# An RMSNorm input laid out twice: a second copy of x with channels on partitions replaces the transposes of three of four token blocks

## The chip, the cores and the metric

One core of a Trainium2 chip. The metric is device time in microseconds of one execution of the kernel; the time of the kernel before is the median of 3 runs.

## The reference

One layer of a streaming-encoder trunk on x of 2048 tokens by 1024 channels, in float32:

```
xn = rmsnorm(x, norm1_g)                  # x * rsqrt(mean(x*x) + 1e-6) * g, per token
z  = xn @ w_in                            # 4608 columns: pool, HGRN2 q / f / i / o, two branch gates
ya = pool_mixer(u) @ w_pa ;  yb = hgrn2(q, f, i, o) @ w_pb
x  = x + (gates_a * ya + gates_b * yb) @ w_o
x  = x + conv_glu_ffn(rmsnorm(x, norm2_g), w_up, conv_w, conv_b, w_down)
return rmsnorm(x, final_g)
```

What matters here is the first line: each token is scaled by its own factor (rstd), each channel by its gain, and the product is needed with channels on partitions, since the projection sums over channels.

## The kernel before, in words

**Blocks.** The tokens are cut into four blocks of 512 (0 to 3), and two blocks make a super-block of 1024 that goes through the mixer and then the FFN (loop at the end of `tile_trunk`, `b` = 0 and 2). The large products over a super-block are done with seven half-size products instead of eight (P1 to P7). Their operands are sums and differences of quarters of the input: B11 and B21 are the first block's channels 0 to 511 and 512 to 1023; T1 to T4 and B22 are formed from both blocks. `forms_a_task` makes B11 and B21 of the even block, `forms_b_task` makes T1 to T4 and B22 of the odd one.

**Precision.** Every operand is split in a high and a low half in fp32r (`split`, L587: high half by ACT L597 or POOL L595, low half by DVE L598), and three matmuls of 128x512 stand for one product. Weights are converted the same way by `stream` (ACT L205, DVE L206), from eight raw buffers that SP loads.

**The input operands.** `load_rows` loads a block as four row tiles of 128 tokens, each in two halves of 512 channels (8 DMAs of 256 KB on SP). `norm_rows` takes a row tile's squares and their sums on ACT (`row_rstd`, L626), the factor rstd on POOL (L627, L619, L620), and multiplies both halves by it on DVE into x_xs (L640). Then 128x128 transposes on PE (L646) bring x_xs into PSUM, 32 for a block. In the even block ACT copies each 128x512 result times the gain into x_b (L654); in the odd block ACT makes -B22 (L714) and DVE the differences t1, t2 and t3 straight from PSUM (`minus`, L703), four each. In block 0 (`early`) the transposes follow row tile by row tile; all others come as the operands are due.

**What sets the order.** The forms are tasks that are stepped once in six matmuls, and the framework's scheduler then fixes one static order for each engine when the kernel is built. An engine carries out its queue in that order: an instruction that waits holds up all behind it. The names: io_X, io_Y, io_Z and io_V are PSUM results of the first part of the input projection (the products with B11, B21, T2 and so on; x_f0 to x_f7 are the split B11 and B21 of the even block); dn_P is the FFN's last product, whose operands dn_P_0h to dn_P_10h and their low halves are cast by ACT (L597) and DVE from tiles g_P. The last product of a super-block (P3, operands 0 to 10) is the work beside which the rows of the next two blocks are loaded and normalised (`X_AT`, `X_AT2` in `ffn`). Tiles come from one pool of 77 slots of 128x528, so a tile's DMA waits until its slot is free.

Of the kernel before, what the change touches and what calls it, by code (L numbers as in the profile page):

```python
# [29 lines left out]
TB = 512  # L30
NT = TB // P
# [26 lines left out]
M_ORDER = (0, 4, 1, 5, 2, 6, 3, 7)  # L58
# [20 lines left out]
def tile_trunk(  # L79
# [10 lines left out]
    w_dn: bass.AP,  # L90
    params: bass.AP,
    final_g: bass.AP,
    out: bass.AP,
):
    nc = tc.nc
    pe, act, dve, pool, sp = nc.tensor, nc.scalar, nc.vector, nc.gpsimd, nc.sync

    const = ctx.enter_context(tc.tile_pool(name="const", bufs=1))
# [395 lines left out]
    xt = {}  # L494
    ready = set()

    def load_x_tile(b, j):
        for c in range(2):
            t = slot(f"x{b}_{j}_{c}")
            r = b * TB + j * P  # L500
            sp.dma_start(t, x[r : r + P, 512 * c : 512 * c + 512])
            xt[("x", b), j, c] = t
        ready.add((("x", b), j))

    def load_rows(b):
        for j in range(NT):
            load_x_tile(b, j)


    load_x_tile(0, 0)  # L510

    ident = const.tile([P, P], F32, tag="ident", name="ident")
# [18 lines left out]
    def col(o):  # L531
        return cols[:, o : o + 1]

    negs = const.tile([P, 16], F32, tag="negs", name="negs")
    pool.tensor_scalar(negs, cols[:, :16], -1.0, None, ALU.mult)

    neghalf = const.tile([P, 4], F32, tag="neghalf", name="neghalf")
    pool.memset(neghalf, -0.5)
# [78 lines left out]
    def rstd_of(ssq, n, scale, name):  # L617
        r = small.tile([P, 4], F32, tag="rstd", name=name)
        pool.tensor_scalar(r[:, :n], ssq, scale, EPS, ALU.mult, ALU.add)  # L619
        pool.tensor_tensor(r[:, :n], r[:, :n], neghalf[:, :n], ALU.pow)  # L620
        return r

    def row_rstd(halves, junk, name):
        ss = small.tile([P, 4], F32, tag="ssq", name=name + "ss")
        for hf in range(2):
            act.activation(junk[hf], halves[hf], AF.Square, accum_out=ss[:, hf : hf + 1])  # L626
        pool.tensor_tensor(ss[:, 2:3], ss[:, 0:1], ss[:, 1:2], ALU.add)  # L627
        return rstd_of(ss[:, 2:3], 1, 1.0 / D, name + "r")

    def norm_rows(src, name, xs, after, lag=1):  # L630
        for j in range(NT):
            while (src, j) not in ready:
                yield 1
            halves = [xt[src, j, c] for c in range(2)]
            t = [slot(f"{name}xs{j}_{hf}") for hf in range(2)]
            r = row_rstd(halves, t, f"{name}{j}")
            if lag:
                yield lag
            for hf in range(2):
                dve.tensor_scalar(t[hf], halves[hf], r[:, 0:1], None, ALU.mult)  # L640
                xs[j, hf] = t[hf]
            after(j)
# [5 lines left out]
    def transposed(xs, k, name, gain, ps=None):  # L648
        if ps is None:
            ps = bank(f"{name}t{k}")  # L650
            for j in range(NT):
                transpose(ps, xs, j, k)
        t = slot(f"{name}b{k}")
        act.activation(t, ps, AF.Copy, scale=col(gain + k))  # L654
        return t
# [10 lines left out]
    def forms_a_task(src, gain, forms, full, after=lambda j: None, early=False):  # L666
        name = f"{src[0]}{src[1]}_"
        xs = {}
        pts = [bank(f"{name}t{k}") for k in range(KD)] if early else [None] * KD

        def rows(j):
            after(j)
            if early:
                for k in range(KD):
                    transpose(pts[k], xs, j, k)

        yield from norm_rows(src, name, xs, rows)
        yield 6
        for k in range(KD):
            t = transposed(xs, k, name, gain, pts[k])  # L680
            yield 1
            key = "B11" if k < 4 else "B21"
            full[key].append(t)
            forms[key].append(split(t, f"{name}f{k}", True))

    def forms_b_task(src, gain, forms, full, after, go):
        name = f"{src[0]}{src[1]}_"
        xs = {}
        yield from norm_rows(src, name, xs, after, 0)
        while not go():  # L690
            yield 2
        t1, b12, b22 = [], [], []

        def turned(k):
            ps = bank(f"{name}t{k}")
            for j in range(NT):
                transpose(ps, xs, j, k)
            return ps

        def minus(key, k, ps, x1, c=None, op=ALU.subtract):  # L700
            t = slot(f"{name}{key}{k}")
            c = gain + (k if c is None else c)
            dve.scalar_tensor_tensor(t, ps, col(c), x1, ALU.mult, op)  # L703
            return t


        t3 = []
        for k in range(4):
            while len(full["B11"]) <= k:
                yield 4  # L710
            p12 = turned(k)
            p22 = turned(k + 4)
            t = slot(f"{name}b{k}")
            act.activation(t, p22, AF.Copy, scale=negs[:, gain + k + 4 : gain + k + 5])  # L714
            b22.append(t)
            t1.append(minus("t1", k, p12, full["B11"][k]))
            t2 = minus("t2", k, p22, t1[k], k + 4)
# [797 lines left out]
    for _ in range(5):  # L1515
        nxt[1].step()
    load_rows(1)
    join(nxt[1])
    Task(setup_task())
# [63 lines left out]
```

## Time and profile before

| | us |
|---|---|
| median of 3 runs | 2624.07 |
| lowest, highest | 2617.74, 2628.94 |
| the profiled execution | 2626.91 |
| its span | 2625.2 |

The span runs from the first to the last instruction; 1.7 us of the profiled execution lie around it. In that execution the granted TensorE clock was 0.987 in the mean. PE was busy for 2537.5 us (97%) of the span, DVE for 1977.9 (75%), ACT for 1170.8 (45%), POOL for 913.0 (35%). Of DMA, 496.90 MB were moved, 189 GB/s in the mean.

How to read the rows in the next sections. A row of a timeline has the start in microseconds from the span's start, the time until its group ended, the engine, the line, the operation, its output and inputs with their shapes, and xN for N such instructions in a row; in brackets stands how long the engine was idle ahead of it and what it waited for. A row of waits has engine, tile and line that waited, the releaser, the total in us, the number of waits and the longest. A row of one line's instructions has the least, median and greatest duration in ns. SPq is SP's queue of DMA issues; its rows give the time of issuing, not of landing.

### The profile page before, as it was taken

What the parts mean: (1) busy time and instruction counts of PE and PEld (TensorE: products, weight loads), DVE (VectorE), ACT (ScalarE), POOL (GpSimd) and SP (SyncE); (2) the same over time, 40 slices, a digit from 0 to 9 for tenths busy, and PEclk for the clock granted to TensorE, in tenths of its full rate; (3) what the DMA queues carried; (4) which work ended last, traced back from release to release, by engine and by line L of the source; (5) the groups of instructions that cost most, each with busy time, mean ns of one, the idle gap of its engine ahead of it and who ended that gap; (6) DMA issues with size and microseconds to landing.
All of it is one profiled execution on the core that took longest, in us unless ns stands there. A gap on an engine that the chain in (4) does not pass through costs nothing. (4 is left out here: it accounts for less than half of the span.)

```text
span 2625.2 us, 35598 instructions
## 1 busy us (share of the span) xinstructions
PE 2537.5 (97%) x11464; PEld 2065.1 (79%) x11464; DVE 1977.9 (75%) x3390; ACT 1170.8 (45%) x2204; POOL 913.0 (35%) x1253
## 2 busy tenths in 40 slices
PE   7899999998999999999999999999999999999998
PEld 6688877777778888878878788888787888887887
DVE  7888779458789877877376787775778887777845
ACT  5334334313655454455364344443345454444633
POOL 6544344042444433353141111210623433335402
PEclk8999999999999999999999999999999999999999
DMA  6787759988768897488364344346452444445942
GB/s 213 271 223 205 204 181 245 267 263 209 217 184 244 239 235 211 148 299 282 98 206 159 97 125 133 109 153 213 149 166 88 151 151 148 141 140 182 378 142 105
DMA packets 254059, 496.90 MB, mean 189 GB/s; under 512 B 26736, under 2 KB 43248, under 8 KB 253552
## 3 DMA queue, kind: packets, MB, share of 16 engines
q1 hardware_dynamic: 187968, 319.89, 38.3%
q0 software_dynamic: 41504, 110.64, 16.5%
q10 hardware_dynamic: 24400, 64.08, 7.0%
q8 instruction: 91, 1.49, 0.2%
q14 instruction: 96, 0.79, 0.1%
HBM read 384.94 MB, written 187.17 MB: 218 GB/s over the span
## 5 line engine op out<-in xcount | busy, mean ns | idle before, releaser
L205 ACT CAST ops<-raw 128x512 fp32r<-128x512 f32 x732 | 451.5, 620 | 819.7 <-PE dn_P L145 140.0
L206 DVE TENSOR_TENSOR ops<-raw,ops 128x512 fp32r<-128x512 f32 x732 | 565.2, 776 | 205.3 <-ACT ops L205 194.3
L1375 DVE SCALAR_TENSOR_TENSOR e<-h,cols,e 128x512 f32<-128x512 f32 x176 | 142.6, 813 | 30.2 <-ACT e L1373 26.1
L1373 ACT ACTIVATE e<-h,cols 128x512 f32<-128x512 f32 x176 | 142.5, 814 | 24.2 <-DVE h L978 16.9
L1378 DVE SCALAR_TENSOR_TENSOR e<-h,cols,e 128x512 f32<-128x512 f32 x176 | 133.9, 769 | 3.0
L796 POOL DMA_DIRECT2D g_P<-dg_P x154 | 83.7, 545 | 107.6 <-PE dn_P L145 69.4
L1084 POOL TENSOR_TENSOR gf_P<-e,e 128x512 f32<-128x512 f32 x44 | 67.9, 1545 | 152.9 <-DVE e L1384 97.5
L1295 POOL TENSOR_TENSOR ya<-ya,gl 128x512 f32<-128x512 f32 x32 | 46.8, 1490 | 107.7 <-DVE gl L1287 107.7
L1084 POOL TENSOR_TENSOR gf_P<-gf_P,e 128x512 f32<-128x512 f32 x44 | 60.2, 1368 | 68.0 <-DVE e L1384 67.5
L1368 POOL COPY h<-h 128x2 f32<-128x2 f32 x88 | 40.7, 481 | 114.3 <-DVE h L976 112.3
L1370 POOL COPY hist<-h 128x2 f32<-128x2 f32 x88 | 35.3, 401 | 125.9 <-DVE h L978 124.2
L1382 ACT ACTIVATE e<-e 128x512 f32<-128x512 f32 x88 | 55.6, 631 | 38.8 <-DVE e L1378 38.4
L1191 POOL TENSOR_TENSOR q<-q,qs 128x512 f32<-128x512 f32 x16 | 21.9, 1366 | 141.6 <-ACT qs L1190 72.9
L978 DVE TENSOR_TENSOR h<-up_u,up_V 128x512 f32<-128x512 f32 x88 | 60.1, 684 | 13.6 <-PE up_V L145 13.1
L1228 ACT ACTIVATE gt<-gt,cols 128x512 f32<-128x512 f32 x48 | 34.8, 725 | 77.4 <-DVE gt L978 63.5
L845 POOL COPY qm<-q 128x64 f32<-128x64 f32 x64 | 24.9, 410 | 117.3 <-DVE q L910 31.2
L1060 DVE TENSOR_TENSOR x<-x,wo_P 128x512 f32<-128x512 f32 x88 | 56.6, 689 | 8.2 <-PE wo_P L145 8.2
L1060 DVE TENSOR_TENSOR ac<-ac,dn_P 128x512 f32<-128x512 f32 x72 | 46.6, 684 | 13.4 <-PE dn_P L145 13.3
L1398 POOL DMA_DIRECT2D dg_P<-gf_P x88 | 52.5, 596 | 10.8 <-POOL gf_P L1084 6.5
L853 PE MATMUL pl<-qm,k 128*128 128x192 f32 x256 | 48.2, 331 | 6.1 <-DVE qm L849 3.8
L1444 POOL TENSOR_TENSOR fss<-fss 128x1 f32<-128x1 f32 x16 | 4.6, 288 | 142.0 <-ACT fj L1433 142.0
L853 PEld LDWEIGHTS pl<-qm,k 128*128 128x128 f32 x256 | 43.3, 191 | 10.4 <-ACT qm L844 3.4
(1265 smaller groups left out, 8283.6 us busy)
## 6 DMA issues: line engine op xcount, KB each, us to landing
g_P<-dg_P POOLq DMA_DIRECT2D x154, 256.0 KB, 6.4
raw<-in_w_up_t SPq DMA_DIRECT2D x132, 256.0 KB, 3.2
raw<-in_w_in_t SPq DMA_DIRECT2D x98, 256.0 KB, 3.2
dg_P<-gf_P POOLq DMA_DIRECT2D x88, 256.0 KB, 3.9
raw<-in_w_io SPq DMA_DIRECT2D x68, 256.0 KB, 5.1
dg_P<-e SPq DMA_DIRECT2D x66, 256.0 KB, 3.3
raw<-in_w_dn SPq DMA_DIRECT2D x66, 256.0 KB, 3.0
x<-in_x SPq DMA_DIRECT2D x64, 256.0 KB, 5.3
```

The costliest lines, as they stand in the source:

```text
L205: self.mark = act.copy(hi, v)
L206: dve.tensor_tensor(lo, v, f32(hi), ALU.subtract)
L796: eng.dma_start(t, d)
L853: pe.matmul(pa_[:, c * 192 : c * 192 + 192], ks[:, (i + c) * P : (i + c + 1) * P], mv[:, c].rearrange("p s x -> p (s x)"), start=True, sto ...
L978: dve.tensor_tensor(dst, t, ps, ALU.add if how == "add" else ALU.subtract)
L1060: dve.tensor_tensor(t, t, ps[j], ALU.add if sg > 0 else ALU.subtract)
L1084: pin(pool.tensor_tensor(t, x0, x1, op))
L1373: in_turn(act.activation(t, h[:, 2:], AF.Identity, bias=col(o_cb + mt), scale=col(o_cw + 4 * MF + mt)))
L1375: in_turn(second(dve.scalar_tensor_tensor(t, h[:, 1 : 1 + TB], col(o_cw + 2 * MF + mt), t, ALU.mult, ALU.add)))
L1378: dve.scalar_tensor_tensor(t, h[:, 0:TB], col(o_cw + mt), t, ALU.mult, ALU.add)
L1382: in_turn(act.activation(g, g, AF.Silu))
L1398: pool.dma_start(d, t)
```

## The change

A second copy of x, transposed on the host ahead of the launch, comes in as the input xc (1024 channels by 2048 tokens). For blocks 1, 2 and 3 `load_rows` also loads the block's eight tiles of 128 channels by 512 tokens (256 KB each), behind the rows. The rows are still loaded, but only for the squares, which now overwrite them. `norm_cols` takes the place of `norm_rows`: from each row tile's rstd, DVE makes a diagonal 128x128 tile (x_di = identity times rstd), PE multiplies a matrix of ones by it (x_rb, fp32), so that each partition holds the 128 factors of the tokens, and when all four are there ACT copies x_rb (128x512) to SBUF as x_rbs. DVE then scales each xc tile in place by the channel's gain and x_rbs. In the even block 2 that is the operand itself; in the odd blocks t1, t2 and t3 are formed from scaled tiles in SBUF, t3 in place, by DVE. Gone for these blocks are x_xs, the transposes (32 a block), ACT's x_b, and the reads of PSUM. Block 0 and the FFN's own norm (m) are unchanged.

```diff
+    ones = const.tile([P, P], F32, tag="ones", name="ones")
+    pool.memset(ones, 1.0)
...
     def load_rows(b):
         for j in range(NT):
             load_x_tile(b, j)
+        if b:
+            for k in M_ORDER if b % 2 else range(KD):
+                t = slot(f"xc{b}_{k}")
+                sp.dma_start(t, xc[k * P : (k + 1) * P, b * TB : (b + 1) * TB])
+                xct[b, k] = t
...
+    def norm_cols(src, name, lag=1):
+
+        ps = bank(f"{name}rb")
+        for j in range(NT):
+            while (src, j) not in ready:
+                yield 1
+            halves = [xt.pop((src, j, c)) for c in range(2)]
+            r = row_rstd(halves, halves, f"{name}{j}")
+            if lag:
+                yield lag
+            t = slot(f"{name}di{j}")[:, :P]
+            dve.tensor_scalar(t, ident, r[:, 0:1], None, ALU.mult)
+            pe.matmul(ps[:, j * P : (j + 1) * P], ones, t, start=True, stop=True)
+        rb = slot(f"{name}rbs")
+        act.copy(rb, ps)
+        return rb
...
     def forms_a_task(src, gain, forms, full, after=lambda j: None, early=False):
...
-        yield from norm_rows(src, name, xs, rows)
-        yield 6
+        rb = None
+        if src[0] == "x" and not early:
+            rb = yield from norm_cols(src, name)
+        else:
+            yield from norm_rows(src, name, xs, rows)
+            yield 6
         for k in range(KD):
-            t = transposed(xs, k, name, gain, pts[k])
+            if rb is None:
+                t = transposed(xs, k, name, gain, pts[k])
+            else:
+                t = xct.pop((src[1], k))
+                dve.scalar_tensor_tensor(t, t, col(gain + k), rb, ALU.mult, ALU.mult)
...
     def forms_b_task(src, gain, forms, full, after, go):
...
-        yield from norm_rows(src, name, xs, after, 0)
+        if src[0] == "x":
+            rb = yield from norm_cols(src, name, 0)
+        else:
+            yield from norm_rows(src, name, xs, after, 0)
...
             else:
-                t3.append(minus("t3", k, p12, b22[k], op=ALU.add))
+                x12, t = (xct.pop((src[1], k + c)) for c in (0, 4))
+                dve.scalar_tensor_tensor(x12, x12, col(gain + k), rb, ALU.mult, ALU.mult)
+                dve.scalar_tensor_tensor(t, t, negs[:, gain + k + 4 : gain + k + 5], rb,
+                                         ALU.mult, ALU.mult)
+                b22.append(t)
+                t1.append(slot(f"{name}t1{k}"))
+                dve.tensor_tensor(t1[k], x12, full["B11"][k], ALU.subtract)
+                t2 = slot(f"{name}t2{k}")
+                dve.scalar_tensor_tensor(t2, t, -1.0, t1[k], ALU.mult, ALU.subtract)
+                dve.tensor_tensor(x12, x12, t, ALU.add)
+                t3.append(x12)
...
+        "xc": a["x"][0].T,
```

The static orders differ from those of before only near the start and near the boundary between the two super-blocks. Three places follow. Line numbers of the changed kernel are 1 to about 50 higher (L206 is L205 of before, L608 is L597, L637 is L626, L682 is L654).

ACT at the start, before, from its fifth cast of weights on (ops<-raw is a weight's high half, x_b an operand of block 0, x_0_0 to x_3_1 in the squares are the row tiles and halves of block 1):

```order
L205 CAST ops_392<-raw_106 128x512
L654 ACTIVATE x_b_230<-x_t_130,cols 128x512
L205 CAST ops_409<-raw_108 128x512
L654 ACTIVATE x_b_236<-x_t_131,cols 128x512
L654 ACTIVATE x_b_242<-x_t_132,cols 128x512
L654 ACTIVATE x_b_248<-x_t_133,cols 128x512
L654 ACTIVATE x_b_254<-x_t_134,cols 128x512
L654 ACTIVATE x_b_260<-x_t_135,cols 128x512
L205 CAST ops_420<-raw_110 128x512
L654 ACTIVATE x_b_266<-x_t_136,cols 128x512
L205 CAST ops_439<-raw_112 128x512
L654 ACTIVATE x_b_272<-x_t_137,cols 128x512
```

The same place after the change, from the sixth cast on:

```order
L206 CAST ops_426<-raw_108 128x512
L637 ACTIVATE x_0_0_216,x_0ss<-x_0_0_216 128x512
L637 ACTIVATE x_0_1_218,x_0ss<-x_0_1_218 128x512
L682 ACTIVATE x_b_248<-x_t_132,cols 128x512
L637 ACTIVATE x_1_0_220,x_1ss<-x_1_0_220 128x512
L637 ACTIVATE x_1_1_222,x_1ss<-x_1_1_222 128x512
L637 ACTIVATE x_2_0_224,x_2ss<-x_2_0_224 128x512
L682 ACTIVATE x_b_254<-x_t_133,cols 128x512
L637 ACTIVATE x_2_1_226,x_2ss<-x_2_1_226 128x512
L637 ACTIVATE x_3_0_228,x_3ss<-x_3_0_228 128x512
L637 ACTIVATE x_3_1_230,x_3ss<-x_3_1_230 128x512
L682 ACTIVATE x_b_260<-x_t_134,cols 128x512
```

The squares of block 1, which stood behind all eight x_b of block 0, now stand ahead of the first and between the next ones; on POOL the statistics of block 1 likewise moved between the splits x_f0h, x_f1h and x_f2h.

ACT at the boundary, before (dn_P_6h and dn_P_7h are operands of the last FFN product of the first super-block; the squares are those of block 2):

```order
L205 CAST ops_12496<-raw_12179 128x512
L597 CAST dn_P_6h<-g_P_6_12164 128x512
L626 ACTIVATE x_xs_0_12378,x_0ss<-x_0_0_12347 128x512
L626 ACTIVATE x_xs_1_12379,x_0ss<-x_0_1_12349 128x512
L626 ACTIVATE x_xs_0_12395,x_1ss<-x_1_0_12351 128x512
L205 CAST ops_12561<-raw_12208 128x512
L626 ACTIVATE x_xs_1_12396,x_1ss<-x_1_1_12353 128x512
L597 CAST dn_P_7h<-g_P_7_12187 128x512
```

And after, from the third row tile of block 2 to that of block 3's end:

```order
L637 ACTIVATE x_2_1_12330,x_2ss<-x_2_1_12330 128x512
L608 CAST dn_P_6h<-g_P_6_12137 128x512
L637 ACTIVATE x_3_0_12332,x_3ss<-x_3_0_12332 128x512
L637 ACTIVATE x_3_1_12334,x_3ss<-x_3_1_12334 128x512
L608 CAST dn_P_7h<-g_P_7_12160 128x512
L608 CAST dn_P_8h<-g_P_8_12166 128x512
```

dn_P_6h stood ahead of all squares of block 2 and now stands behind the sixth of the eight, with dn_P_7h and dn_P_8h behind the last.

ACT a little later, after the change (x_rbs is of block 2, the squares are of block 3):

```order
L655 COPY x_rbs<-x_rb 128x512
L206 CAST ops_12707<-raw_12365 128x512
L637 ACTIVATE x_0_0_12465,x_0ss<-x_0_0_12465 128x512
L637 ACTIVATE x_0_1_12467,x_0ss<-x_0_1_12467 128x512
L637 ACTIVATE x_1_0_12469,x_1ss<-x_1_0_12469 128x512
L637 ACTIVATE x_1_1_12471,x_1ss<-x_1_1_12471 128x512
L637 ACTIVATE x_2_0_12473,x_2ss<-x_2_0_12473 128x512
L637 ACTIVATE x_2_1_12475,x_2ss<-x_2_1_12475 128x512
L637 ACTIVATE x_3_0_12477,x_3ss<-x_3_0_12477 128x512
L608 CAST dn_P_9h<-g_P_9_12243 128x512
L637 ACTIVATE x_3_1_12479,x_3ss<-x_3_1_12479 128x512
```

Before, dn_P_9h stood ahead of block 3's squares and dn_P_10h behind the eighth; now dn_P_9h is behind the seventh, and dn_P_10h follows the copy x_rbs of block 3. On PE dn_P_10's matmuls moved behind the first matmuls of io_X, and x_rb's four stand between dn_P_6 and dn_P_8 for block 2 and from dn_P_9 on for block 3. On SP, block 2's eight xc loads stand between the rows of block 2 and five raw weights, and block 3's rows and xc tiles stand behind three more raw weights (kw0ioP to kw2ioP); before, block 3's rows stood behind one.

More of the change, by code (lines that the diff above doesn't have):

```diff
@@ L92, in tile_trunk @@
     final_g: bass.AP,
+    xc: bass.AP,
     out: bass.AP,
@@ L503, in load_x_tile @@
         ready.add((("x", b), j))
+    xct = {}
     def load_rows(b):
@@ L710, in forms_b_task @@
                 yield 4
[L711 to L717, printed above, removed]
-            if src[0] == "m":
+            if src[0] == "m":
+                p12 = turned(k)
+                p22 = turned(k + 4)
+                t = slot(f"{name}b{k}")
+                act.activation(t, p22, AF.Copy, scale=negs[:, gain + k + 4 : gain + k + 5])
+                b22.append(t)
+                t1.append(minus("t1", k, p12, full["B11"][k]))
+                t2 = minus("t2", k, p22, t1[k], k + 4)
                 t = slot(f"{name}t3{k}")
@@ L722, in forms_b_task @@
             else:
-                t3.append(minus("t3", k, p12, b22[k], op=ALU.add))
+                x12, t = (xct.pop((src[1], k + c)) for c in (0, 4))
+                dve.scalar_tensor_tensor(x12, x12, col(gain + k), rb, ALU.mult, ALU.mult)
+                dve.scalar_tensor_tensor(t, t, negs[:, gain + k + 4 : gain + k + 5], rb,
+                                         ALU.mult, ALU.mult)
+                b22.append(t)
+                t1.append(slot(f"{name}t1{k}"))
[4 more added lines that the diff above has]
+                t3.append(x12)
             forms["T2"].append(split(t2, f"{name}T2{k}"))
```

## The prediction

> **What bounds the kernel now.** I read the page first, then busy time by stretch, PE's waits in two of the stretches, then those places instruction by instruction.
>
> ```profile
> span 2625.2 us, 35598 instructions
> PE 2537.5 (97%) x11464; PEld 2065.1 (79%) x11464; DVE 1977.9 (75%) x3390; ACT 1170.8 (45%) x2204; POOL 913.0 (35%) x1253
> PE   7899999998999999999999999999999999999998
> PEclk8999999999999999999999999999999999999999
> ```
> ```profile
> 7.60:130.00 122.40, 106.32 (x443) 84.64 (x444) 105.20 (x138) 55.75 (x108) 73.89 (x90) 0.93 0.71 243
> 1320.00:1390.00 70.00, 64.70 (x299) 52.45 (x298) 56.30 (x90) 44.16 (x99) 28.79 (x48) 0.95 0.58 195
> ```
>
> PE is busy for 97% of the span, so what counts is PE's queue and its few waits. In the second fence the columns are length, then PE, PEld, DVE, ACT and POOL busy, granted clock, DMA share and GB/s. Those two stretches (the start, and the boundary between the super-blocks) lose 16.1 and 5.3 us of PE time and have the low clocks. All transposes of x lie in them, so the change is priced there. PE's waits in the first, then in the second:
>
> ```profile
> PE x_t L646 <- DVE x_xs L640: 8.7, 3, 7.6
> PE io_Z L145 <- DVE io_u L1129: 3.8, 1, 3.8
> PE x_t L646 <- DVE x_t L703: 3.6, 2, 2.1
> PE io_X L145 <- POOL x_f0h L595: 2.4, 1, 2.4
> PE io_Z L145 <- DVE x_t L703: 1.5, 1, 1.5
> ```
> ```profile
> PE dn_P L145 <- ACT dn_P_10h L597: 3.6, 1, 3.6
> PE dn_P L145 <- ACT dn_P_7h L597: 1.0, 1, 1.0
> ```
>
> 7.6 of the 8.7 us is the wait before PE's first instruction. The transposes of block 1 then cost waits of 1.1 + 3.6 + 1.5 = 6.2 us. The wait for io_u comes later in the start, and is a wait for DVE whatever PE did before.
>
> **What the change takes off PE.** 96 transposes of the 128 of x (block 0 keeps 32).
>
> ```profile
> 1361.66 1.04 PE L646 MATMUL x_t<-ident,x_xs 128*128 128x128 f32 x8
> 1362.45 0.71 PE L145 MATMUL io_Y<-ops,x_f5h 128*128 128x512 f32 x2
> L892 PE MATMUL pl<-q,k x256: 270/275/461, 147.1 to 1725.5; 128*128 128x128 f32 x128
> ```
>
> Eight take (1362.45 - 1361.66) = 0.79 us of queue, 0.1 each, so 96 are 9.5 us. Twelve matmuls x_rb come in. The nearest row is the fp32 128x128 matmul pl (median 275 ns, neighbours overlapping): between 0.1 and 0.27 each, 1.2 to 3.3 us; I take 0.12, the transpose's end, since a lone transpose has the same duration (0.27 us). So PE has 8 us less to do. That is a gain only where PE gets its operands sooner.
>
> **The start.**
>
> ```profile
> 13.97 0.68 ACT L654 ACTIVATE x_b<-x_t,cols 128x512 f32<-128x512 f32 x1
> 15.06 3.00 ACT L654 ACTIVATE x_b<-x_t,cols 128x512 f32<-128x512 f32 x5
> 10.73 5.06 SPq L501 DMA_DIRECT2D x<-in_x  x8
> x<-in_x SPq DMA_DIRECT2D x64, 256.0 KB, 5.3
> 17.17 1.04 POOL L595 TENSOR_SCALAR x_f2h<-x_b 128x512 fp32r<-128x512 f32 x1
> 16.67 2.07 PE L145 MATMUL io_X<-ops,x_f0h 128*128 128x512 f32 x4 [2.41 <-POOL x_f0h L595]
> 29.43 0.62 PE L145 MATMUL io_Y<-ops,x_f4h 128*128 128x512 f32 x2
> 40.56 1.47 PE L646 MATMUL x_t<-ident,x_xs 128*128 128x128 f32 x12
> 52.22 1.22 PE L145 MATMUL io_Z<-ops,x_T20h 128*128 128x512 f32 x2 [1.53 <-DVE x_t L703]
> ```
>
> In the new order two squares of block 1 stand on ACT ahead of block 0's first x_b, and six more among the next ones. They wait for DMAs: the second load is issued at about 10.7 + 0.65 and lands 5.3 later, at 16.7. With its square (0.6) x_b starts at 17.4 instead of 13.97, and x_f0h, 1.04 on POOL, ends at about 19.2: the first matmul of io_X comes at 19.2 for 16.67, **2.5 us later**. Then PE has half of io_X (24 matmuls) and stands before x_rb, whose x_di is on DVE behind x_f7l. POOL makes the eight splits of 1.04 and, between them, three more rows' statistics (about 1 us each): 18.1 + 11.3 = 29.5, and x_f7l 0.7 more: 30.2. PE waits about 3 us there. A matmul takes (40.56 - 29.43)/48 = 0.232 at full clock; after a wait the first four took 2.07, 0.52 each, so the clock is halved and some 1.7 us more go. The rest of io_X (5.6 + 1.7 + 0.7 for x_rb and the step in) ends at 38.2, io_Y 11.1 later at 49.4, for 40.56. From here the gain: the stretch from 40.56 to 52.22, 11.7 us of transposes and their waits, is gone, and io_Z starts at about 49.4 rather than 52.22.
>
> The Trainium skill (TensorE: Matmul & The Clock Gate, Part 1) has the clock fall only after an idle window of about 3.4 us. By that my 3 us wait costs no half clock, and the sum would be 1.7 us less; the row after a 2.41 us wait (0.52 each) speaks against it.
>
> PE's lead of 3 us is not kept, for DVE sets the end of this stretch.
>
> ```profile
> L703 DVE SCALAR_TENSOR_TENSOR x_t<-x_t,cols,x_b x8: 736/742/746, 43.4 to 55.5; 128x512 f32<-128x512 f32 x8
> L640 DVE TENSOR_SCALAR x_xs<-x,x_0r x4: 480/484/487, 7.1 to 37.7; 128x512 f32<-128x512 f32 x4
> L206 DVE TENSOR_TENSOR ops<-raw,ops x16: 678/680/1764, 11.7 to 127.7; 128x512 fp32r<-128x512 f32 x16
> 92.09 1.19 PE L145 MATMUL io_Z<-ops,x_T40h 128*128 128x512 f32 x2 [3.79 <-DVE io_u L1129]
> ```
>
> Off DVE go 8 x_xs (0.48) and 12 L703 (0.74): 12.7 us. On it come 4 x_di (not in the trace; between 0.1 and 0.48 as they have a quarter of x_xs's columns; 0.2 taken), 12 scalar_tensor_tensors at 0.74 and 8 tensor_tensors at 0.68: 15.1. So DVE has 2.4 us more, of which the 0.08 that starts overlap take some 1. Its place for the eight scalings is after x_rbs (ACT's copy, about 36.7), and it idles from 31 to there, as it idled about as long at 22 to 31 before. Contention adds some more (rival 2). So io_u, and PE at 92.09, come 1.5 us later; PE's wait of 3.8 grows by its lead. Bounds: -3 if the scalings fit into DVE's idle time, +5 if a third of the 20 operations take the 1.76 us that the L206 row has as its maximum. **Start: +1.5 us.**
>
> ```profile
> 16.17 3.58 SPq L182 DMA_DIRECT2D raw<-in_w_io  x6
> 31.09 1.29 POOL L338 TENSOR_TENSOR w8s<-raw,raw 128x512 f32<-128x512 f32 x1
> ```
>
> On SP's queue the eight loads of xc stand ahead of these six raw weights, which land 5.4 us later: the first at 16.2 + 5.3 + 5.4 = 26.9, the last at 30.5. Their first reader, w8s, ran at 31.09, so this is hidden by less than a microsecond; w8s itself moves behind the later x_f7h in any case.
>
> **The boundary.**
>
> ```profile
> 1318.58 0.62 ACT L597 CAST dn_P_6h<-g_P 128x512 fp32r<-128x512 f32 x1
> 1322.51 0.63 ACT L626 ACTIVATE x_xs<-x 128x512 f32<-128x512 f32 x1 [3.32 <-DMA x<-in_x]
> 1341.18 0.60 ACT L597 CAST dn_P_10h<-g_P 128x512 fp32r<-128x512 f32 x1
> 1320.67 3.55 SPq L501 DMA_DIRECT2D x<-in_x  x5
> 1323.33 2.03 PE L145 MATMUL dn_P<-ops,dn_P_6h 128*128 128x512 f32 x8
> 1341.84 3.78 PE L145 MATMUL dn_P<-ops,dn_P_10h 128*128 128x512 f32 x8 [3.60 <-ACT dn_P_10h L597]
> 1375.36 0.71 PE L145 MATMUL io_Z<-ops,x_T20h 128*128 128x512 f32 x2 [0.30 <-DVE x_t L703]
> ```
>
> Before, the cast dn_P_6h stood ahead of block 2's squares and was done at 1319.2; dn_P_10h stood behind all squares of block 3, and PE waited 3.60 us for it. Now dn_P_6h stands behind the sixth square of block 2, dn_P_9h behind the copy x_rbs and seven squares of block 3.
> - dn_P_6h: the sixth load is the third of the five from 1320.67 on, issued at about 1322.1 and landed 5.3 later, 1327.4 to 1327.7. Square and cast: PE starts dn_P_6 at 1328.9 for 1323.33. That is 5.6 us of waiting, and half clock behind it (8 in 3.78 against 8 in 2.03): 1.7.
> - dn_P_6 to 8 are 36 matmuls, 8.4, with the 1.7 and four x_rb: PE is through at about 1339.6.
> - dn_P_9h: x3's rows are loaded behind the eight new loads of xc (256 KB, 3.55/5 = 0.7 each): 5.4 us later. Block 3's squares ended at 1341.18, so the eighth would end at 1346.6, the seventh at 1346, and PE starts dn_P_9 at about 1346.5: 6.9 us of waiting, 1.7 of half clock. Its low half stands on DVE behind the eight scalings of block 2, which x_rbs releases at about 1337: done by 1343, so ACT is the later one. The raw weights of the next projection, also 5.4 us later, are first used behind io_X's start and stay hidden.
> - dn_P_9 and dn_P_10, io_X, io_Y: 24 + 96 matmuls, 27.9; with 1.7 and 0.5 for x_rb, io_Z starts at 1376.6.
> Before, 1375.36: **boundary +1.2 us**. Bounds: -9 if the squares never hold the casts (5.6 + 6.9 + 2 x 1.7 gone, and DVE's eight scalings, 5.3, late instead); +6 if x3's loads also wait for raw buffers that PE frees late, or the half clock lasts twice as long.
>
> Elsewhere ACT loses 16 x_b and POOL nothing; ACT is 45% busy and hides that. The 6 MB more of DMA lie in these two places.
>
> **Sum.** +1.5 + 1.2 = +2.7 on the profiled execution: 2625.2 + 2.7, and the 1.7 us that lay around the span, make 2629.6. That execution was 2.8 above the median of 2624.07, so on the median's scale it is 2626.8; I give 2628, between.
>
> **Rivals.**
> 1. *The squares hold up nothing* (the loads land sooner, or casts find operands ready). For it: ACT is idle 55% of the time. Against: ACT waited 3.32 us for the very load of x. Then the boundary is -9 and the start -3: 2612 to 2615. Chance 0.10 for over 0.5% faster (13 us, about what a measurement tells from no change).
> 2. *DVE and POOL collide*, the slower side. Before, L703 read one operand from PSUM; all 20 new operations of a b-block read two from SBUF. L206, which does so too, takes 0.68, but 1.76 at most. POOL makes its sums of weights in just that stretch of the start. If each of block 1's 20 pays 1.08, PE at 92.09 is 21 us later: 2648. It decides from 10 of the 20 on (+11 beside the 2.7). Chance 0.12.
> 3. *Boundary at its upper bound*, +6: 2634. Chance 0.10; it lies within 0.5%.
>
> The Trainium skill (SBUF — State Buffer, Who interferes with whom) has a Vector instruction with two SBUF inputs and a GpSimd instruction that reads SBUF exclude each other for a whole instruction. By that rule each of the 20 that meets a POOL sum pays, as rival 2 has it; the median of 0.68 says that most do not meet one.
>
> The forecast itself has 0.68. Faster 0.10, the same 0.78, slower 0.12. The range reaches from rival 1's upper edge to most of rival 2's: 2613 to 2644.
>
> **What would show it.** Right: 5 to 6 us of PE waiting for dn_P_6h and 6 to 7 for dn_P_9h, with ACT waiting for x's DMA ahead of both; no wait of 3.6 for dn_P_10h; io_X starting 2.5 us later and io_Z about 3 earlier in the start; PE's wait for io_u above 3.8. Wrong: x_b at 14 as before, or xc's scalings well over 0.74 each, or a gain over 5 us, which would mean that the orders on ACT cost nothing.

## The result, and the profile after

The changed kernel takes 2648.28 us (median of 6 runs) where the kernel before takes 2627.42 (median of 6): the ratio is 1.0083, with a 95% interval from 1.0069 to 1.0097. Forecast were 2628 us and no change that can be measured; the time lies 4 us above the top of the range. The profiled execution took 2647.6 us, and its span is 20.7 us longer than that of before.

The page of the changed kernel, the span, the busy times and the rows of PE and its clock:

```profile
span 2645.9 us, 35450 instructions
PE 2537.2 (96%) x11392; PEld 2061.2 (78%) x11392; DVE 1979.4 (75%) x3402; ACT 1162.5 (44%) x2191; POOL 924.8 (35%) x1254
PE   6899999898999999999979999999999999999998
PEclk8999999999999999999989999999999999999999
```

PE executes 72 instructions fewer than the 11464 of before: 96 transposes are gone, but the twelve products x_rb show as 24 instructions, two each. For all that, PE is busy as long as before: read in windows of 2 us, the granted clock is at half for 78.6 us of this span and for 61.4 of that of before, and 17.2 us at half clock cost up to 8.6 us of busy time, about what the missing work would have saved. The 20.7 us are time in which PE waits. The rows of PE and of its clock have a new dip at the 21st slice, which is the boundary between the super-blocks. The two stretches of the prediction, in the changed kernel (length; PE, PEld, DVE, ACT, POOL busy; clock, DMA share, GB/s):

```profile
7.60:130.00 122.40, 99.27 (x392) 76.67 (x392) 101.61 (x136) 53.68 (x104) 75.37 (x90) 0.90 0.71 241
1320.00:1390.00 70.00, 53.60 (x216) 42.36 (x215) 47.16 (x74) 32.82 (x78) 27.90 (x49) 0.88 0.70 238
```

In the second, PE now loses 16.4 us of 70 (before: 5.3), at a clock of 0.88 (0.95). PE's waits there:

```profile
PE dn_P L146 <- ACT dn_P_9h L608: 8.7, 1, 8.7
PE dn_P L146 <- ACT dn_P_6h L608: 5.4, 1, 5.4
PE io_Z L146 <- ACT x_T21h L608: 1.7, 1, 1.7
PE io_Z L146 <- ACT x_T20h L608: 1.5, 1, 1.5
PE io_Y L146 <- DVE ac L1109: 0.8, 1, 0.8
```

Together 18.1 us up to 1400 us (the last 1.7 lie behind the stretch), where before they were 3.6 + 1.0. And in the start:

```profile
PE io_Z L146 <- DVE io_u L1178: 6.2, 1, 6.2
PE io_X L146 <- POOL x_f0h L606: 5.2, 1, 5.2
PE x_rb L653 <- DVE x_di L652: 3.1, 1, 3.1
```

**Where the 20.7 us arise** is read from landmarks: PE instructions that both programs have and that wait for the same thing. In the changed kernel they stand at

```profile
98.33 1.19 PE L146 MATMUL io_Z<-ops,x_T40h 128*128 128x512 f32 x2 [6.19 <-DVE io_u L1178]
...
1137.88 0.96 PE L146 MATMUL dn_P<-ops,dn_P_3h 128*128 128x512 f32 x3 [1.75 <-ACT dn_P_3h L608]
...
1474.48 0.57 PE L941 MATMUL pl<-q,k 128*128 128x128 f32 x3 [1.21 <-DVE q L869]
...
2430.21 0.50 PE L146 MATMUL dn_P<-ops,dn_P_3h 128*128 128x512 f32 x1 [1.75 <-ACT dn_P_3h L608]
```

and before the last three stood at

```profile
1131.53 0.96 PE L145 MATMUL dn_P<-ops,dn_P_3h 128*128 128x512 f32 x3 [1.75 <-ACT dn_P_3h L597]
...
1457.31 0.46 PE L892 MATMUL pl<-q,k 128*128 128x128 f32 x2 [1.22 <-DVE q L820]
...
2409.04 1.01 PE L145 MATMUL dn_P<-ops,dn_P_3h 128*128 128x512 f32 x2 [1.75 <-ACT dn_P_3h L597]
```

The first stood at 92.09. The difference is 6.2 us at the first landmark, 6.35 at the second, 17.2 at the third, 21.2 at the fourth, 20.7 at the end. So the **start** costs 6.2 us (forecast 1.5), the **boundary** 10.8 (forecast 1.2), and the second super-block, in which nothing was changed, 4.0. Between the first two landmarks nothing was changed either: 1039.4 us before, 1039.6 after. In the profiles of all versions this stretch has 1035.1 to 1043.8 us, so a few microseconds of a whole time say little about an edit, and the landmarks say more.

### The profile page after: what moved, and what is told of

Read it like the earlier page. It is cut to its first block, busy times and chain, and to the rows that moved or that the text cites. A ratio compares the mean times of both kernels' runs of the same rounds, so it can differ in the third digit from the quotient of the medians.

```text
span 2645.9 us, 35450 instructions
## 1 busy us (share of the span) xinstructions
PE 2537.2 (96%) x11392; PEld 2061.2 (78%) x11392; DVE 1979.4 (75%) x3402; ACT 1162.5 (44%) x2191; POOL 924.8 (35%) x1254
## 5 line engine op out<-in xcount | busy, mean ns | idle before, releaser
L206 ACT CAST ops<-raw 128x512 fp32r<-128x512 f32 x732 | 451.7, 620 | 835.9 <-PE dn_P L146 154.8
L1447 POOL DMA_DIRECT2D dg_P<-gf_P x88 | 52.5, 596 | 10.8 <-POOL gf_P L1133 6.5
L902 PEld LDWEIGHTS pl<-qm,k 128*128 128x128 f32 x256 | 43.2, 191 | 10.5 <-issue 4.4
```

The lines of the kernel that those rows point to most:

```text
L206: self.mark = act.copy(hi, v)
L902: pe.matmul(pa_[:, c * 192 : c * 192 + 192], ks[:, (i + c) * P : (i + c + 1) * P], mv[:, c].rearrange("p s x -> p (s x)"), start=True, sto ...
```

## The experiments

Two theories were set against each other. *Order* (the first): the loss comes from where things stand in the in-order queues; block 1's squares ahead of block 0's x_b at the start, and the squares and x_rbs of blocks 2 and 3 ahead of the last dn_P casts on ACT. *DVE* (the rival): the loss comes from what DVE now has to do, twenty operations a b-block with two operands in SBUF, which collide with POOL, and the copy x_rbs that makes them so. The texts on record use these names. All ratios are to the kernel before on the same chip; its medians there were 2626.3 to 2628.5 us.

**Which block costs what.** `b1_old` treats block 1 as before (rows, x_xs, transposes) and blocks 2 and 3 in the new way; `b23_old` is the reverse, with `{2, 3}`.

```diff
+OLD = {1}
...
-        if b:
+        if b and b not in OLD:
...
-        if src[0] == "x" and not early:
+        if src[0] == "x" and not early and src[1] not in OLD:
...
-        if src[0] == "x":
+        if src[0] == "x" and src[1] not in OLD:
...
```

> Block 1 is normalised and transposed as before; blocks 2 and 3 use the second copy of x. Theory Order (the loss is made where squares that wait for x's DMAs, and scalings that wait for x_rbs, stand in an engine's queue ahead of work that was ready): the start is as before (PE at io_u's release at 92 us, not 98), the boundary keeps its waits of about 5.4 us for dn_P_6h and 8.7 us for dn_P_9h, and the time is 11 to 15 us above the kernel before, ratio 1.004 to 1.006. Theory DVE (the two-SBUF-operand work on DVE, slowed by POOL, is the loss): the loss goes with the number of such operations, and most of them meet POOL in block 1's stretch: ratio 1.002 or less.

> Blocks 2 and 3 as before; block 1 alone uses the second copy of x. Theory Order: the start loses 6 us (PE at 98 us where it was at 92), the boundary is as before with a wait of 3.6 us for dn_P_10h; ratio about 1.0025 (1.001 to 1.004). Theory DVE: most of the loss of 21 us is here, ratio 1.006 or more. With the run that has block 1 as before, the two losses should add up to that of the whole change (21 us) by either theory.

Measured: `b1_old` 1.0052 (1.0033 to 1.0071), 2637.51 us; `b23_old` 1.0021 (1.0009 to 1.0032), 2631.77. That is 11.2 and 5.5 us, and each profile shows its own half: `b1_old` has PE at io_Z at 93.71 in the start (before: 92.09) and waits of 5.7 and 8.5 for dn_P_6h and dn_P_9h; `b23_old` has io_Z at 97.24 and at the boundary waits of 3.9 for dn_P_10h and 0.9 for dn_P_7h, nearly as before. The two places add up to 16.7 of the 20.7 us.

**The start: order alone.** `start_sq` is the changed kernel with block 1's squares put behind block 0's last x_b on ACT.

```diff
+            i = act.activation(junk[hf], halves[hf], AF.Square, accum_out=ss[:, hf : hf + 1])
+            if name[:3] == "x1_":
+                behind(i, last_b[0])
...
+        last_b[0] = act.activation(t, ps, AF.Copy, scale=col(gain + k))
```

> The changed kernel with one order altered: block 1's squares stand on ACT behind all eight x_b of block 0. Theory Order: x_b starts at 14 us as before, io_X at 16.7, x_rbs by about 31 instead of 38.4, so DVE's first scaling comes some 7 us earlier and PE is at io_u's release at about 92: 6 us of the 21 come back, ratio 1.0055 (1.004 to 1.007). Theory DVE: the scalings and sums still take the same time beside POOL, so io_u stays 4 us or more late and the ratio is 1.007 or more.

Measured: 1.0071 (1.0047 to 1.0096), 2641.34 us. The interval is too wide to tell it from the changed kernel by time; the profile tells it:

```profile
92.71 1.19 PE L146 MATMUL io_Z<-ops,x_T40h 128*128 128x512 f32 x2 [6.20 <-DVE io_u L1182]
```

io_Z stands at 92.71 for 98.33, with nearly the same DVE work and the same scalings from SBUF: 5.6 of the start's 6.2 us are order. Other profiles give the size of chance here: with the order of the changed kernel io_Z stands at 96.5 to 98.9 in five (`after`, `after_again`, `b23_old`, `early_rows`, `xc_last`), with the squares behind x_b at 92.7 and 94.3 (`start_sq`, `early_both`). How it works is seen in DVE's busy time (third number behind the length) ahead of 22 us and from there to io_u. Before, after, and in `start_sq`:

```profile
7.60:22.00 14.40, 11.77 (x48) 10.02 (x49) 11.89 (x19) 10.16 (x22) 9.63 (x15) 0.88 1.05 396
22.00:92.10 70.10, 60.27 (x258) 47.83 (x256) 61.07 (x85) 33.41 (x65) 39.05 (x58) 0.92 0.58 197
```
```profile
7.60:22.00 14.40, 9.02 (x39) 7.65 (x40) 7.88 (x16) 12.72 (x33) 7.33 (x19) 0.80 1.05 390
22.00:98.30 76.30, 62.20 (x243) 47.16 (x241) 67.13 (x93) 29.29 (x52) 42.81 (x55) 0.90 0.62 208
```
```profile
7.60:22.00 14.40, 12.01 (x50) 10.58 (x51) 12.44 (x20) 13.66 (x31) 9.80 (x17) 0.88 1.04 388
22.00:92.70 70.70, 56.84 (x232) 42.77 (x231) 61.55 (x89) 27.75 (x52) 42.76 (x57) 0.97 0.66 225
```

DVE's idle time from 22 us on is the same before and after: 70.1 - 61.07 = 9.0 and 76.3 - 67.13 = 9.2 us. Ahead of 22 it does 7.88 us of work instead of 11.89. It waits there for the high halves of block 0's operands; before, then in the changed kernel:

```profile
16.65 1.09 DVE L598 TENSOR_TENSOR x_f0l<-x_b,x_f0h 128x512 fp32r<-128x512 f32 x1 [0.51 <-POOL x_f0h L595]
```
```profile
19.19 0.69 DVE L609 TENSOR_TENSOR x_f0l<-x_b,x_f0h 128x512 fp32r<-128x512 f32 x1 [3.07 <-POOL x_f0h L606]
21.47 0.69 DVE L609 TENSOR_TENSOR x_f1l<-x_b,x_f1h 128x512 fp32r<-128x512 f32 x1 [1.59 <-POOL x_f1h L606]
```

Those 4.0 us are never made up; with the squares behind x_b they are not lost. DVE's work as a whole grows by 2.05 us (75.01 for 72.96).

**The boundary: rows and squares earlier.** `early_rows` loads the rows of blocks 2 and 3 and takes their squares and x_di during the product ahead of the last (P4), when ACT has time; the xc tiles are loaded where the rows were, and x_rb is made when they come.

```diff
+        def each4(k):
+            if k == 2 and not last:
+                load_rows(b0 + 2)
...
+            if k == 6 and not last:
+                load_rows(b0 + 3)
+
         def each3(k):
             if k == X_AT and not last:
-                load_rows(b0 + 2)
...
+                load_cols(b0 + 2)
             if k == X_AT2 and not last:
-                load_rows(b0 + 3)
+                load_cols(b0 + 3)
...
-        down.run("P4", 2, done=lambda j: Task(final(0, j)))
         go_io[0] = False
+        down.run("P4", 2, each4, done=lambda j: Task(final(0, j)))
...
-        ps = bank(f"{name}rb")
+        di = []
...
-            pe.matmul(ps[:, j * P : (j + 1) * P], ones, t, start=True, stop=True)
+            di.append(t)
+        while (src[1], 0) not in xct:
+            yield 1
+        ps = bank(f"{name}rb")
+        for j in range(NT):
+            pe.matmul(ps[:, j * P : (j + 1) * P], ones, di[j], start=True, stop=True)
```

> The changed kernel with the rows of blocks 2 and 3 loaded, squared and turned into x_di about 25 to 30 us earlier, during the product before; their xc tiles are loaded where the rows were. Theory Order: ACT's casts no longer stand behind squares that wait for a DMA, the waits of 5.4 and 8.7 us for dn_P_6h and dn_P_9h go, and 10 to 17 of the 21 us come back: ratio 1.0015 to 1.004. Theory DVE: the 16 scalings and 12 sums of these blocks are the same, so at most the casts' waits go and come back as waits for DVE: ratio 1.006 or more.

Measured: 0.9977 (0.9966 to 0.9987), 2618.45 us: faster than before, and better than either theory expected. Between the second and third landmark lie 316.0 us (changed kernel 336.6, before 325.8). The waits of 5.4 and 8.7 for ACT are gone, and so is the wait of 3.6 that the kernel before had in the same place; the longest left at dn_P is one of 1.2 for dn_P_8l.

Theory DVE does not account for it: the eight scalings of block 2 even took longer (0.96 us each in the mean, 0.79 in the changed kernel), the other new operations there as long, and the loss is gone all the same.

`early_both` has both edits. 

> Both orders mended: block 1's squares behind block 0's x_b, and the rows of blocks 2 and 3 loaded and squared during the product before. Theory Order: the two repairs add: about 6 us below the run with early rows alone (0.9977), ratio 0.995 to 0.997, faster than the kernel before, since the transposes' PE time and waits at the boundary are then really gone. Theory DVE: at the start the DVE work stays, so nothing adds: 0.9975 or more.

Measured: 0.996 (0.9947 to 0.9973), 2616.33 us; start and boundary at 94.34 and 316.4.

**What DVE's operand is worth.** `psum_rb` is the changed kernel with the scalings reading x_rb in PSUM, without the copy; `early_psum` is the same edit on top of `early_both`.

```diff
-        rb = slot(f"{name}rbs")
-        act.copy(rb, ps)
-        return rb
+        return ps
```

> The changed kernel with only this: scalings read x_rb from PSUM, no copy x_rbs. Theory Order: the waits for dn_P_6h (5.4) and dn_P_9h (8.7) and the late x_b stay; 1 to 3 us come back, ratio 1.007 to 1.008. Theory DVE: the 24 scalings no longer collide, 8 us or more come back: 1.005 or lower.

> As the run with both orders mended, and the scalings read x_rb from PSUM instead of the copy x_rbs, so they have one operand in SBUF; ACT's copy is gone. Theory Order: x_rb is ready 1 us sooner and one or two scalings of 1.78 us fall back to 0.75: 1 to 3 us less than with the copy at most, or nothing. Theory DVE (collisions of two-operand reads with POOL are the loss): 6 us or more less than with the copy, ratio 0.993 or lower.

Measured: `psum_rb` 1.0047 (1.0033 to 1.006), 2639.27 us: 9 us less than the changed kernel, which is the number of theory DVE, and a miss for Order (1.007 to 1.008). But the profile gives that number mostly another reason. In the start, where io_Z stands 3.2 us earlier, the scalings begin 1.6 us earlier since no copy precedes them, and none collides with work on POOL, which saves 2.1; one t2 now takes 1.67 us instead of 0.69, which takes 1.0 back. In the changed kernel, and then in `psum_rb`:

```profile
38.40 0.59 ACT L655 COPY x_rbs<-x_rb 128x512 f32<-128x512 f32 x1 [0.99 <-PE x_rb L653]
39.02 0.75 DVE L763 SCALAR_TENSOR_TENSOR xc<-xc,cols,x_rbs 128x512 f32<-128x512 f32 x1 [0.88 <-ACT x_rbs L655]
41.68 1.78 DVE L763 SCALAR_TENSOR_TENSOR xc<-xc,cols,x_rbs 128x512 f32<-128x512 f32 x1
44.71 1.79 DVE L764 SCALAR_TENSOR_TENSOR xc<-xc,negs,x_rbs 128x512 f32<-128x512 f32 x1
```
```profile
37.42 0.75 DVE L761 SCALAR_TENSOR_TENSOR xc<-xc,cols,x_rb 128x512 f32<-128x512 f32 x1 [0.27 <-PE x_rb L653]
1361.04 1.09 DVE L609 TENSOR_TENSOR dn_P_10l<-g_P,dn_P_10h 128x512 fp32r<-128x512 f32 x1
```

At the boundary dn_P_6h and dn_P_9h are waited for as before (5.6 and 8.1), but the three waits at io_Y and io_Z (0.8 + 1.5 + 1.7) are gone or 0.3, and the stretch between the landmarks is 4.7 us shorter (331.9). The scheduler, which no longer has the copy to place, put dn_P_10l ahead of block 3's eight scalings on DVE; in the changed kernel it stands behind them, 9 us later (the row is below). That this order is what removed the waits is read from the two profiles; no run changes it alone. So this edit, meant for collisions, changed an order too. `early_psum` took 2611.97 us, 0.9941 (0.9929 to 0.9954): 4.4 us under `early_both`, between what the two theories expected, and the fastest kernel of all. io_Z of the start stands at 90.36 for 94.34, and here collisions do count: in `early_both` block 1's eight scalings took 8.9 us together, in `early_psum` 5.9.

**Block 3's rows ahead of the channels.** `xc_last` loads the xc tiles of both blocks behind the rows of both.

```diff
                 load_rows(b0 + 3)
+                load_cols(b0 + 2)
+                load_cols(b0 + 3)
```

> The changed kernel with the xc tiles of blocks 2 and 3 loaded behind the rows of both. Theory Order: dn_P_6h stands behind three squares only, whose rows land first, so its wait falls from 5.4 to about 1; block 3's rows are no longer behind eight loads of xc but still behind raw weights that wait for PE, and dn_P_9h stands behind all eight squares: its wait stays at 4 to 8. About 5 us come back: ratio 1.005 to 1.007. Theory DVE: no change, 1.008.

Measured: 1.0046 (1.003 to 1.0061), 2637.45 us. A half miss: PE waits

```profile
PE dn_P L146 <- ACT dn_P_9h L610: 10.5, 1, 10.5
PE dn_P L146 <- ACT dn_P_6h L610: 0.9, 1, 0.9
```

The second fell as expected. The first was to stay at 4 to 8 us, behind all eight squares of block 3, and is longer. The order of loads does not remove the waits for squares that stand ahead of a cast; of the edits that keep the second copy of x, those with the squares one product earlier on ACT (`early_rows` and the versions with it) did.

**Was it the transposes at all?** `before_early` is the kernel before, with its transposes, and rows and norms of blocks 2 and 3 early as in `early_rows`.

```diff
+    turn = {0}
...
+        while src[0] == "x" and src[1] not in turn:
+            yield 1
...
+        def each4(k):
+            if k == 2 and not last:
+                load_rows(b0 + 2)
...
+            if k == 6 and not last:
+                load_rows(b0 + 3)
+
         def each3(k):
             if k == X_AT and not last:
-                load_rows(b0 + 2)
...
+                turn.add(b0 + 2)
```

> The kernel before, with its transposes, but with the rows of blocks 2 and 3 loaded, squared and scaled into x_xs during the product before, as in the runs with early rows. If the gain of those runs comes from the early rows alone, this has it too: ratio 0.994 to 0.996. If the 64 transposes of these blocks and their waits are worth their PE time as well (6 to 7 us, by 0.1 us each), it stands between: the waits of 1.0 and 3.6 us and the half clock go, 5 to 8 us, ratio 0.997 to 0.998.

Measured: 0.9963 (0.9949 to 0.9977), 2615.31 us, with no wait at dn_P and 316.9 us between the landmarks. At the boundary the gain of the early versions is nearly all that of the early rows. With these, the removal of the transposes is worth 316.9 - 316.0 = 0.9 us there (`early_rows`), and 316.9 - 312.8 = 4.1 with the PSUM operand (`early_psum`). `early_rows` and `early_both` have one stretch of 3.4 us at half clock there that the other two lack, which is up to 1.7 us of the difference. In the start, where `before_early` is as before (io_Z at 92.09), the new way is 2.3 us later in `early_both` and 1.7 earlier in `early_psum`. Of whole times, `early_both` can't be told from `before_early`, and `early_psum`'s interval just overlaps that of `before_early`.

**Less work on DVE.** `early_t3pool` is `early_psum` with t3 formed by POOL.

```diff
-                dve.tensor_tensor(x12, x12, t, ALU.add)
+                pool.tensor_tensor(x12, full["B11"][k], t2, ALU.subtract)
```

> The fastest run so far (both orders mended, x_rb read from PSUM), with the four t3 of each odd block made by POOL instead of DVE. If DVE's plain work sets the start's end, PE at io_u's release comes 1 to 2.5 us earlier than 90.4: ratio 0.993 to 0.994. If POOL's new operations (1.4 us each) collide with DVE's, it is the same or later: 0.994 to 0.996.

Measured: 0.9956 (0.9942 to 0.997), 2615.84 us, no better: io_Z of the start stands at 91.28 for `early_psum`'s 90.36, where 1 to 2.5 us earlier was hoped for. The t3 took 1.5 us each on POOL. Why nothing was gained was not followed further.

**The 4 us of the second super-block.** `after_again` is the changed kernel, unchanged.

> The changed kernel, nothing altered, to see what of the 21 us is left over after the start (6.2) and the boundary (10.8): in the first profile the stretch from the second super-block's first wait for q (1474.5) to its dn_P_3h (2430.2) took 955.7 us against 951.7 before, with half-clock windows that the profile of before does not have there. If these 4 us belong to the change, the stretch takes 955 to 956 again. If the windows fall by chance, it takes 950 to 954 as in the other runs, and the time varies by as much from run to run: ratio 1.006 to 1.008.

Measured: 1.0067 (1.0053 to 1.0081), 2647.05 us. The stretch between the last two landmarks is 955.7 us again (before: 951.7). The longer time comes with stretches of lower clock that before lacks there. In the changed kernel, and before:

```profile
1915.00:1950.00 35.00, 32.79 (x128) 25.75 (x129) 27.97 (x47) 6.21 (x10) 0.00 (x0) 0.90 0.39 128
2004.00:2039.00 35.00, 30.61 (x113) 22.36 (x112) 30.08 (x43) 18.04 (x32) 13.93 (x16) 0.90 0.22 68
```
```profile
1900.00:1935.00 35.00, 33.16 (x142) 26.72 (x143) 28.46 (x48) 10.03 (x22) 1.95 (x6) 1.00 0.47 152
1985.00:2020.00 35.00, 30.24 (x123) 22.10 (x122) 32.00 (x45) 20.48 (x35) 15.38 (x17) 1.00 0.23 76
```

PE is about as busy and does fewer matmuls, 0.9 of the clock. All profiles together, with the clock read in windows of 2 us, say that the length of this stretch goes with the clock:

| half clock between the last two landmarks, us | length of the stretch, us | profiles |
|---|---|---|
| 3.4 | 950.8 to 952.3 | before and seven versions |
| 6.8 | 951.0 | `xc_last` |
| 10.2 | 953.4 | `start_sq` |
| 13.7 | 954.6 | `early_t3pool` |
| 17.1 | 955.7 | the changed kernel, twice |

So it is no property of the second copy of x alone: `b1_old` and `b23_old`, which have half of it each, show 3.4, and `early_t3pool`, without the waits at the boundary, 13.7. Whether every execution of the changed kernel has it is not known: two of its eleven runs took 2640 us, at a mean clock of 0.987 for 0.982 to 0.985 in the others, and these two have no profile. In the changed kernel the two long stretches set in at waits of 2.0 and 1.8 us, which before has too (1.6 and 1.8). What decides whether the clock falls there stays open.

## Why the prediction was wrong, point by point

**Held.** The half clock even after short waits (3.06 us ahead of x_rb), x_b and io_X 3.3 and 2.5 us later (17.28 and 19.21 in the changed kernel, 17.4 and 19.2 forecast), and PE's waits for x_rb and dn_P_6h:

```profile
19.21 1.22 PE L146 MATMUL io_X<-ops,x_f0h 128*128 128x512 f32 x2 [5.17 <-POOL x_f0h L606]
30.87 0.77 PE L653 MATMUL x_rb<-x_di,ones 128*128 128x128 f32 x2 [3.06 <-DVE x_di L652]
1335.02 3.78 PE L146 MATMUL dn_P<-ops,dn_P_6h 128*128 128x512 f32 x8 [5.41 <-ACT dn_P_6h L608]
```

3.06 us (forecast about 3) and 5.41 (5.6). The wait for io_u grew, from 3.8 to 6.2, as it should. The mechanism was right, and the size of the sum was lost in two terms, the start and the boundary; the 4 us of the second super-block had no term.

**PE's lead in the start, about 3 us forecast, 1.1 measured.** io_Z starts at 51.15 (forecast 49.4, before 52.22):

```profile
51.15 2.00 PE L146 MATMUL io_Z<-ops,x_T20h 128*128 128x512 f32 x8
```

x_rb came 0.7 us later than forecast, and the half clock behind its wait, priced at 1.7 us, lasted from 29.7 to 36.5, which costs PE half of the 5.7 us that it works in it, 2.8. As the prediction said, this lead is not kept, so the sum does not suffer by it.

**The start, +1.5 forecast, +6.2 measured.** The step that failed is "So io_u, and PE at 92.09, come 1.5 us later". It took DVE's new work (2.4, measured 2.05) and compared DVE's idle time between 22 us and the scalings in both programs, which are about as long (7.6 and 8.6 us from 22 to 39). It left out the idle time ahead of 22: the 3.3 us by which block 0's x_b come later, which the prediction itself had worked out for PE, also hold up DVE's low halves of the same operands. On PE the removed transposes made up for that delay; DVE is busy for 88% of the time from there to io_u, and sets the end. 4.0 of idle and 2.05 of work are 6.1 of the 6.2 us, and `start_sq` shows the first: with the order of before, it is gone.

That 2.4 and 2.05 agree is luck. By their durations, the new operations took 18.8 us (15.1 forecast; three of them were slow, and x_di took 0.28 to 0.47 each) and the ones that went 14.0 (12.7), so 4.8 more. The rest of DVE's work in the start changed too: its 28 low halves of operands fell from 27.2 to 24.5 us and its eight casts m from 3.8 to 1.6, while others rose.

**The boundary, +1.2 forecast, +10.8 measured.** Put on the scale of before (6.35 us subtracted), the working goes wrong little by little. PE starts dn_P_6 at 1328.7 (forecast 1328.9) and is through with dn_P_8 at 1340.7 (1339.6): the half clock lasted longer, twelve matmuls instead of eight, and each x_rb is two instructions. Then it starts dn_P_9 at 1349.4 (1346.5): the wait is 8.7, not 6.9. The step that failed here is "x3's rows are loaded behind the eight new loads of xc [...]: 5.4 us later". The timelines of SP and of ACT in the changed kernel tell why:

```profile
1341.91 0.33 SPq L183 DMA_DIRECT2D raw<-kw1ioP  x1
1344.95 0.32 SPq L183 DMA_DIRECT2D raw<-kw2ioP  x1
1345.32 3.74 SPq L502 DMA_DIRECT2D x<-in_x  x8
```
```profile
1348.38 0.63 ACT L637 ACTIVATE x<-x 128x512 f32<-128x512 f32 x1 [0.72 <-DMA x<-in_x]
1355.06 0.60 ACT L608 CAST dn_P_9h<-g_P 128x512 fp32r<-128x512 f32 x1
```

Block 3's rows are issued 0.4 us after the weight kw2ioP ahead of them on SP, and seven squares later comes the cast. SP's two waits at the last weights are for raw buffers that DVE has not yet read, and ACT's casts of earlier weights wait for operand buffers that PE, itself waiting, has not freed; from the waits of SP, then of ACT:

```profile
SPq L183 <- DVE ops L207: 4.8, 2, 2.6
```
```profile
ACT ops L206 <- PE dn_P L146: 5.7, 2, 3.3
```

This is the mechanism of the prediction's upper bound, not its chosen value. The prediction counted only the eight xc loads ahead of these rows (at its own 0.7 each they make 5.6, not 5.4) and gave the three raw weights, which the orders ahead of it name, no time. How much each of these waits adds is read from the profile and was not tried one by one.

The rest is lost behind dn_P_9. From there to io_Z the forecast was 30.1 us, and the timelines of PE and of DVE have 33.9:

```profile
1355.71 3.78 PE L146 MATMUL dn_P<-ops,dn_P_9h 128*128 128x512 f32 x8 [8.71 <-ACT dn_P_9h L608]
1389.59 2.12 PE L146 MATMUL io_Z<-ops,x_T20h 128*128 128x512 f32 x8 [1.52 <-ACT x_T20h L608]
```
```profile
1370.49 0.69 DVE L609 TENSOR_TENSOR dn_P_10l<-g_P,dn_P_10h 128x512 fp32r<-128x512 f32 x1
```

io_Z starts 7.9 us later than before, and waits once more for x_T21h. No price was set for most of this: DVE carries dn_P_10l behind block 3's scalings, so the additions to ac and the operands of io_Z come late, 0.8 + 1.5 us of waiting ahead of io_Z and 1.7 behind its start. `psum_rb`, which has dn_P_10l at 1361.04, has nearly none of it. The half clock, again twelve matmuls long, has about 0.8 more of the 3.8. Up to io_Z 2.9 + 3.8 = 6.7 us were missed, and behind it 2.9 more, of which 1.7 is the wait for x_T21h; 1.2 are not assigned.

**Rival 2**, collisions at +21 us, has nearly the measured time (2648) and is not the cause. Two of block 1's eight scalings and one t1 took 1.76 to 1.79 us, so 3 of the 20 operations and not all of them, 3.2 us in the start. Other work of DVE became shorter, so that all of it grew by 2.05. In `start_sq` three of the 20 are slow as well, and 5.6 us come back. The Trainium skill (SBUF — State Buffer, Who interferes with whom) says that a VectorE instruction with two SBUF inputs contends with a GpSimd instruction that reads SBUF, and that one with at most one SBUF input, outside the 2-port modes, does not. The scalings agree (up to 1.79 us from SBUF, none of 48 above 0.75 with x_rb in PSUM), but few met one.

**PE's saving** was overstated: 8 us, with 0.12 for each of twelve x_rb. There are 24 instructions in the trace at about that pitch, so some 6.6 us. At the boundary that makes 64 x 0.1 - 16 x 0.12 = 4.5; `early_psum`, with 0.8 us of waiting there and no half clock, shows 4.1.

**Rival 1's** two bounds, -9 and -3, add up to 12 us, a little less than the 13 that its chance is stated for.

## What to carry to other kernels

On in-order queues, price a delay on every engine that reads the delayed operand, not only on the one that waits first: the engine that is saturated afterwards keeps all of it. Work that waits for a DMA (here the squares) belongs where its engine's queue has nothing urgent behind it; moving it one product earlier took 8.9 us off the boundary of the kernel with transposes (325.8 to 316.9) and 20.6 off that of the one without (336.6 to 316.0), while the transposes themselves are worth 1 to 4 us of it. And an edit that takes an instruction away lets a scheduler reorder the rest, so that its gain is read from the new order first.

## What the runs showed that was not expected

The half clock comes in whole steps. Cut into windows of 0.1 us, the granted clock of the changed kernel is at half from 29.7 us for 6.83 us, from 1333.6 for 6.83 and from 1350.7 for 10.24; in `xc_last` it is so for 17.1 us around the wait of 10.5. All are multiples of 3.41. The first belongs to a wait of only 3.06 us and sets in 1.9 us after PE's last matmul ended, and those at the boundary set in some 4 us into PE's waits of 5.4 and 8.7 and outlast the eight matmuls that the prediction allowed. The Trainium skill (TensorE: Matmul & The Clock Gate, Part 1) has a free-running window of about 3.4 us, with which the steps agree; that a pause shorter than the window can be followed by the lower clock is not what it leads one to expect.

So in these three places a wait of PE cost its own length and then half of what was left of two or three such steps behind it: 2.8 us behind the wait of 3.06, and about 2.6 for twelve matmuls behind each of the other two.

A fp32 128x128 product shows as two matmul instructions in the trace, where a transpose of the same size shows as one:

```profile
L653 PE MATMUL x_rb<-x_di,ones x24: 272/276/553, 30.9 to 1363.6; 128*128 128x128 f32 x24
```
